# Two projection blocks in one PSUM bank, urgent marks on the delta rule's chain, and tied splits of the last weights

## The chip, the cores and the metric

The kernel runs on one core of a Trainium2 chip. TensorE (PE) does the matrix products, VectorE (DVE) and ScalarE (ACT) the elementwise work, GpSimd (POOL) some fills, and SyncE (SP) issues most DMAs. Every engine takes its instructions in the order of its own queue and waits on semaphores that others raise. The metric is device microseconds of one launch, the median of several runs.

## The reference

One layer of a hybrid network on 256 tokens of 2048 features, all in fp32:

```python
h = rms_norm(x, attn_norm_w)
proj = h @ w_in                       # 3360 columns for the RWKV half, 3088 for the delta rule's half
y_a = rwkv7_mixer(proj[..., :N_RWKV_IN], ...)       # token shift, low-rank gates, recurrence over tokens
y_b = gdn_mixer(proj[..., N_RWKV_IN:], ...)         # causal conv of 4 taps, gated delta rule in chunks of 64
x = x + concat([y_a, y_b]) @ w_out
h = rms_norm(x, ffn_norm_w)
x = x + (silu(h @ ffn_w_gate) * (h @ ffn_w_up)) @ ffn_w_down      # 5632 inner columns
return rms_norm(x, final_norm_w)
```

The delta rule walks four chunks in order. In each it forms the new values from the state `S`, adds to the output, and updates `S`, so that a chunk can't begin before the one ahead has left its state. At its end stand a norm of each head, a transpose and a product with `silu(z)`.

## The kernel before, in words

**Weights.** All weights come as fp32 tiles of 128x1024 (512 KB). Each is split into a high part `wh`, a rounded copy made by ACT, and a low part `wl`, the rest, made by DVE; three products (high by high, high by low, low by high) stand for one in fp32. `load_split` (L177) issues the DMA on SP's queue and the split. There are three buffers `raw` and two each of `wh` and `wl`. `split` (L244, lines L246 and L247) takes a whole tile at once; `halves_of` (L194, lines L202 and L203) takes it in two halves, for the FFN.

**First projection.** `proj_in` (L309) makes one column block of 128 output features for 256 tokens: two weight tiles, for the two halves of the 2048 inputs, each with 24 matmuls in `products` (L214: 16 that use `wh`, then 8 that use `wl`). The block fills 256 of the 512 fp32 columns of one PSUM bank, tag `pb`, of which there are two. `evac_norm` (L228, line L232) multiplies the block by `rstd` into one of two buffers `pr`, and a token shift (L238, L239) or a conv of four taps (L667, L669) follows. Blocks come in pairs, `m` = 0 and 1, which fill the two halves of one tile `t`, `outt` or `z`: twelve pairs in `rwkv_stream` (L649), eight in `conv_silu` (L660), four in the loop over `z` (L982), the last of which, `last2`, is built in two banks.

**Side work.** The recurrences are generators. `tick` (L165) is called after each step of `products` and carries each generator as far as its condition lets it, so that its instructions stand between the products in program order. `gdn` (L748) holds the delta rule: `tri_inverse` (L336), then four chunks. In a chunk: `psK` = keys and queries by the state (L898), eight corrections of `vn` (L903), `psUg` (L911), scaled copies (L915, L917), `psSg` for the new state (L923, then L928 or L932), `psOg` (L938, L942, L944), and, after every second chunk, squares with sums (L949), an inverse root (L951, L139 to L143) and a scaling (L954). The last steps transpose to `ps_og` (L964) and write `yg` (L967). Then follow the splits of the four `ys` tiles (L1008), the right-hand sides of the next projection.

**Second projection.** `w_out` is gone through twice (L1015): `q` = 0 for all 16 column blocks needs the RWKV outputs `yR` alone, `q` = 1 needs `yg`.

**FFN.** Eleven units of 512 inner columns, each with a gate and an up product (`gate_up`, L1049, 8 weight tiles and 96 matmuls of 128x512 each) and two `down` (L1134, 4 tiles and 48 matmuls each). The last unit's `down` weights are split ahead of time into SBUF places that others have left: within `gate_up` of the unit at column 36 (b = 0 and 2), at every even `kk` a tile is loaded to the one buffer `raw_end` (L1062), and at the next odd `kk` `halves_of(raw, own)` splits it (L1057, rows named `wend`). These are eight tiles, four in the gate and four in the up product.

**What sets the order.** The kernel is written in program order, and the tile framework's scheduler puts each engine's queue together at build time by simulating the machine: of the instructions that are ready in its model, the one with the lowest priority number goes first. The number is the place in program order; within `hi()` (L60) it is lowered by a million, so that `hi` work goes ahead of all other, and among `hi` work the earlier in the program first. Loads and splits of weights and the evacuations of the projections are `hi`; the delta rule's chain is not. `together` (L63) adds edges that keep a list of instructions in order on their engine; an edge without a semaphore only fixes the order.

Of the kernel before, what the change touches and what calls it, by code (L numbers as in the profile page):

```python
# [49 lines left out]
def trunk_kernel(ctx, tc, xT, vecs, fnw, w_up, a_up, g_up, w_in, w_ab, w_out, w_gu, w_dn, out):  # L50
# [9 lines left out]
    def hi():  # L60
        return tc.high_priority(offset=HI)

# [131 lines left out]
    def halves_of(raw, places, by_k=False):  # L194
        parts = []
        r4 = raw.rearrange("p (c k f) -> p k c f", c=4, k=2)
        for h in range(2):
            wh, wl = places()
            src, oh, ol = raw[:, h * 512:h * 512 + 512], wh, wl
            if by_k:  # L200
                src, oh, ol = r4[:, h], wh.rearrange("p (c f) -> p c f", c=4), wl.rearrange("p (c f) -> p c f", c=4)
            S.activation(oh, src, AF.Copy)  # L202
# [23 lines left out]
    prn = [0]  # L226

    def evac_norm(ps):  # L228

        prn[0] += 1  # L230
        pr = prs[prn[0] % 2]
        V.tensor_tensor(pr[:, 4:260], ps[:, 0:T], rstd, ALU.mult)  # L232
        return pr

    def evac_shift(ps, mu, out):
        with hi():
            pr = evac_norm(ps)
            S.activation(out, pr[:, 4:260], AF.Copy, scale=vec[:, mu + OMU:mu + OMU + 1])  # L238
            shifted[0] = V.scalar_tensor_tensor(out, pr[:, 3:259], vec[:, mu:mu + 1], out, ALU.mult, ALU.add)  # L239
        return pr  # L240
# [68 lines left out]
    def proj_in(cb):  # L309
        return proj([(w_in[cb, q], xk[8 * q:8 * q + 8]) for q in range(2)])  # L310

# [6 lines left out]
    for i in range(2):  # L318
        evac_shift(ps_first[i], VEC["mu_l"] + i, pl[:, i, :])
# [329 lines left out]
    def rwkv_stream(hf):  # L649
        for gr in range(2):  # L650
            for i, (d, mu, tag, nb) in enumerate(((kt, "mu_k", "kt", 2), (rt, "mu_r", "rt", 2), (vt, "mu_v", "vt", 4))):
                f = hf * 4 + gr * 2
                t = rp.tile([P, 2, T], F32, tag=tag, name=f"{tag}{hf}{gr}", bufs=nb)
                for m in range(2):
                    evac_shift(proj_in(2 + ((hf * 2 + gr) * 3 + i) * 2 + m), VEC[mu] + f + m, t[:, m, :])
                vready[(hf, gr)] = shifted[0]
                d[(hf, gr)] = t


    def conv_silu(ti, b0, outt):  # L660
        for m in range(2):
            ps = proj_in(2 * ti + m)
            tb = outt[:, m, :]
            with hi():
                pr = evac_norm(ps)
                c0 = (b0 + m) * 4
                S.activation(tb, pr[:, 4:260], AF.Copy, scale=vc("conv", c0 + 3))  # L667
                for i in range(3):
                    V.scalar_tensor_tensor(tb, pr[:, 1 + i:257 + i], vc("conv", c0 + i), tb, ALU.mult, ALU.add)  # L669
# [78 lines left out]
    def gdn():  # L748
# [136 lines left out]
        for ch in range(NCH):  # L885
# [5 lines left out]
            if ch:  # L891
# [10 lines left out]
                for h in range(8):  # L902
                    ready.append(V.scalar_tensor_tensor(vn[rows, cp, h, :],  # L903
# [13 lines left out]
            ready = [S.copy(vn[rows, cp, m::2, :], u3[m * 64:m * 64 + 64]) for m in range(2)]  # L917
            yield None
            mo, news = [], []
            if ch < NCH - 1:  # L920
# [5 lines left out]
                for i in range(2):  # L926
                    if ch == 0:
                        news.append(S.copy(Sg[:, 4 * i:4 * i + 4, :].rearrange("p h f -> p (h f)"), psS[i]))  # L928
                    else:
                        for j in range(4):  # L930
                            h = 4 * i + j
                            news.append(V.scalar_tensor_tensor(Sg[:, h, :], Sg[:, h, :], egc[:, h, ch:ch + 1],  # L932
# [8 lines left out]
            for m in range(2):  # L941
                S.activation(vn[rows, cp, m::2, :], o3[m * 64:m * 64 + 64], AF.Copy, scale=-1.0)  # L942
            for h in range(8 if ch else 0):
                V.scalar_tensor_tensor(vn[rows, cp, h, :], psK[h // 4][rq, h % 4 * P:h % 4 * P + P],  # L944
                                        GTn[rq, cp, h:h + 1], vn[rows, cp, h, :], ALU.mult, ALU.add)
            if x:
                ss, rs, xh = [rsg[:, o + 8 * cp:o + 8 * cp + 8] for o in (0, 16, 32)]
                for h in range(8):
                    S.activation(junk, vn[:, cp, h, :], AF.Square,  # L949
                                 accum_out=ss[:, h:h + 1])  # L950
                V.scalar_tensor_tensor(xh.rearrange("p (h x) -> p h x", x=2), ss.rearrange("p (h x) -> p h x", x=2),  # L951
                                       0.5 / 128, nq[:, cp::2, None].to_broadcast([P, 4, 2]), ALU.mult, ALU.add)
                rsqrt(rs, xh, "g")
                scaled = [S.activation(vn[:, cp, h, :], vn[:, cp, h, :], AF.Copy, scale=rs[:, h:h + 1])  # L954
# [11 lines left out]
        for i, ps in enumerate(pss):  # L966
            V.scalar_tensor_tensor(yg[:, 2 * i:2 * i + 2, :].rearrange("p h t -> p (h t)"), ps, vc("gnw"),  # L967
# [14 lines left out]
    for i in range(4):  # L982
# [66 lines left out]
    def gate_up(c0, m, tag="pb", beside=None):  # L1049
# [243 lines left out]
```

## Time and profile before

| | us |
|---|---|
| median of 3 runs | 1256.54 |
| lowest and highest | 1255.93, 1258.83 |
| the profiled execution, whole | 1255.44 |
| its span in the profile | 1253.7 |
| first matmul of the second projection (`psb` from `ys`) | 397.97 |
| first matmul of the FFN (`psq`) | 510.03 |

The span is counted from the first instruction to the last; 1.7 us lie around it. Up to about 398 us PE works on the first projection with the recurrences between, up to 510 us on the second, and then on the FFN. The profile's page gives busy time by engine; of the trace, the views used below are the busy time in windows, the waits of one engine, the chain of work that ended last, the timeline of one engine, and the groups of instructions by line. In a timeline, the columns are start and duration in us, engine, line, operation, tiles (written, then read), shapes and count, and in brackets the idle time before it and what ended that.

### The profile page before, as it was taken

The numbers are of one execution on the slowest core, as the hardware profiler recorded it, in microseconds if no ns is written. First come the engines' busy times: TensorE is split into PE (matmuls) and PEld (weight loads), VectorE is DVE, ScalarE is ACT, GpSimd is POOL, SyncE is SP. The second block draws the span as 40 slices with busy tenths as digits, with TensorE's granted clock in tenths as the row PEclk, the third lists the DMA queues.
The fourth block names the chain that finished last, engine by engine and source line by source line (L and its number), as shares of the span: only waits on it lengthen the run. The fifth ranks groups of instructions, "written<-read, shape, count | busy, mean of one in ns | idle before, by whom it ended". The sixth has DMA issues, their size and how long they took to land.

```text
span 1253.7 us, 21133 instructions
## 1 busy us (share of the span) xinstructions
PE 1234.8 (98%) x8134; PEld 1087.0 (87%) x8134; DVE 834.3 (67%) x1635; ACT 651.3 (52%) x1199; POOL 17.8 (1%) x63
## 2 busy tenths in 40 slices
PE   8999999999999999999999999999999999999997
PEld 8999999999999989888888888888888888878886
DVE  7987887977966877565555555555656565665554
ACT  7575665667546456554444444444444444454443
POOL 3000000000000000000000000000000000000000
PEclk9999999999999999999999999999999999999999
DMA  7455665575573445676666666666676666676641
GB/s 248 153 169 179 169 170 149 169 186 139 196 213 118 145 159 186 172 205 194 190 190 197 188 193 192 194 190 196 187 198 182 189 190 195 203 236 193 193 151 67
DMA packets 175702, 226.68 MB, mean 181 GB/s; under 512 B 52273, under 2 KB 144561, under 8 KB 175345
## 3 DMA queue, kind: packets, MB, share of 16 engines
q1 hardware_dynamic: 170896, 221.54, 60.4%
q10 hardware_dynamic: 4560, 2.74, 0.8%
q8 instruction: 64, 1.05, 0.4%
q0 software_dynamic: 144, 1.05, 0.2%
q14 instruction: 38, 0.30, 0.1%
HBM read 218.75 MB, written 4.46 MB: 178 GB/s over the span
## 4 chain that ended last, share of the span: by engine, by line
PE 88%; DVE 5%; DMA 3%; issue 1%; ACT 1%; SPq 0%; ACTq 0%; DVEq 0%
PE psq L1070 37%; PE psd L1147 17%; PE psb L220 16%; PE psb L223 8%; DVE wl L247 2%; PE psT L1102 1%; DMA sX_r<-X_r 1%; DMA raw_end<-in_w_dn 1%; DMA st_r<-sX_r 1%; PE ps_A L485 1%; PE psd L1198 1%; PE psd L1196 1%; PE psd L1197 1%; DMA A_g<-sG 0%; PE psSg L923 0%
## 5 line engine op out<-in xcount | busy, mean ns | idle before, releaser
L203 DVE TENSOR_TENSOR wl<-raw,wh 128x512 fp32r<-128x512 f32 x524 | 340.7, 692 | 273.5 <-ACT wh L202 271.8
L202 ACT ACTIVATE wh<-raw 128x512 fp32r<-128x512 f32 x524 | 302.5, 626 | 363.9 <-PE psq L1070 192.4
L1070 PE MATMUL psq<-wh,x2s 128*128 128x512 f32 x1408 | 377.4, 390 | 0.8 <-ACT wh L202 0.8
L1070 PEld LDWEIGHTS psq<-wh,x2s 128*128 128x128 f32 x1408 | 263.7, 188 | 56.2 <-ACT wh L202 1.7
L1070 PE MATMUL psq<-wl,x2s 128*128 128x512 f32 x704 | 217.2, 389 | 0.0
L220 PE MATMUL psb<-xs,wh 128*128 128x256 f32 x816 | 206.4, 287 | 2.4 <-ACT wh L202 1.7
L223 PE MATMUL psb<-xs,wh 128*128 128x256 f32 x816 | 206.0, 286 | 0.0
L1147 PE MATMUL psd<-wh,h 128*128 128x512 f32 x640 | 203.2, 391 | 1.0 <-ACT wh L202 1.0
L246 ACT ACTIVATE wh<-raw 128x1024 fp32r<-128x1024 f32 x128 | 135.4, 1058 | 87.4 <-PE psb L223 67.8
L247 DVE TENSOR_TENSOR wl<-raw,wh 128x1024 fp32r<-128x1024 f32 x128 | 156.1, 1220 | 11.1 <-ACT wh L246 10.9
L220 PEld LDWEIGHTS psb<-xs,wh 128*128 128x128 f32 x816 | 156.8, 192 | 4.4 <-ACT wh L202 2.4
L223 PEld LDWEIGHTS psb<-xs,wh 128*128 128x128 f32 x816 | 156.8, 192 | 1.2 <-issue 0.7
L1070 PEld LDWEIGHTS psq<-wl,x2s 128*128 128x128 f32 x704 | 132.0, 188 | 27.6
L1147 PEld LDWEIGHTS psd<-wh,h 128*128 128x128 f32 x640 | 119.2, 188 | 25.8 <-ACT wh L202 1.7
L220 PE MATMUL psb<-xs,wl 128*128 128x256 f32 x816 | 127.1, 287 | 0.9 <-DVE wl L247 0.7
L1147 PE MATMUL psd<-wl,h 128*128 128x512 f32 x320 | 124.6, 389 | 0.0
L220 PEld LDWEIGHTS psb<-xs,wl 128*128 128x128 f32 x816 | 109.8, 192 | 2.8 <-DVE wl L247 1.1
L1147 PEld LDWEIGHTS psd<-wl,h 128*128 128x128 f32 x320 | 60.1, 188 | 12.7
L223 PE MATMUL psb<-ys,wh 128*128 128x256 f32 x256 | 64.6, 288 | 2.5 <-DVE ys L247 2.5
L220 PE MATMUL psb<-ys,wh 128*128 128x256 f32 x256 | 64.8, 289 | 0.2 <-ACT ys L246 0.2
L223 PEld LDWEIGHTS psb<-ys,wh 128*128 128x128 f32 x256 | 50.1, 196 | 2.8 <-DVE ys L247 2.7
L1155 DVE TENSOR_TENSOR acc<-acc,psd 128x512 f32<-128x512 f32 x80 | 49.5, 682 | 1.8 <-PE psd L1147 1.8
(315 smaller groups left out, 1026.8 us busy)
## 6 DMA issues: line engine op xcount, KB each, us to landing
raw<-in_w_gu SPq DMA_DIRECT2D x176, 512.0 KB, 4.9
raw<-in_w_in SPq DMA_DIRECT2D x99, 512.0 KB, 3.5
raw<-in_w_dn SPq DMA_DIRECT2D x80, 512.0 KB, 4.3
raw<-in_w_out SPq DMA_DIRECT2D x32, 512.0 KB, 3.5
raw_end<-in_w_dn SPq DMA_DIRECT2D x8, 512.0 KB, 4.2
xraw<-in_xT SPq DMA_DIRECT2D x8, 256.0 KB, 5.8
x<-in_xT SPq DMA_DIRECT2D x1, 2048.0 KB, 9.7
raw<-in_w_ab SPq DMA_DIRECT2D x2, 512.0 KB, 4.9
```

The costliest lines, as they stand in the source:

```text
L202: S.activation(oh, src, AF.Copy)
L203: V.tensor_tensor(ol, src, oh, ALU.subtract)
L220: PE.matmul(ps[:, 0:T], w, rt[:, ri, 0:T], start=(first and k == 0 and not low), stop=(last and k == 7 and low == 1))
L223: PE.matmul(ps[:, 0:T], w, rt[:, ri, T:], start=False, stop=False)
L246: S.activation(hi_ap, src, AF.Copy)
L247: V.tensor_tensor(lo_ap, src, hi_ap, ALU.subtract)
L485: PE.matmul(psA[h][:, ch, :], bk[hr, ch].rearrange("p a t -> p (a t)"), ar[hr, p, ch].rearrange("p a t -> p (a t)"), start=True, stop=True)
L1070: last = PE.matmul(banks[tb], t[:, ri, o + tb * P:o + tb * P + P], w, start=(k == 0 and o == 0 and w is wh), stop=(k == KB - 1 and w is wl))
L1102: ms.append(PE.transpose(ps[b][:, o:o + P], sg[tb][:, (2 * b + i) * P:(2 * b + i) * P + P], ident))
L1147: m = PE.matmul(banks[tb * 2 + cg], st, parts[cg][w], start=(i == 0 and w == 0 and st is hh), stop=(i == n - 1 and st is hl))
L1155: V.tensor_tensor(acc[:, tb, cs], acc[:, tb, cs], banks[tb * 2 + cg], ALU.add)
L1196: PE.matmul(ps, hh, wh, start=(i == 0), stop=False)
```

## The change

Three things are changed.

1. `proj_in2` builds the two blocks of a pair in the two halves of one bank, the first block whole and then the second. One `evac_norm` of 128x512 takes both to one buffer `prs` of two halves. The shifts and convs, and the `z` product, then follow for both. `last2` stays as it was. The buffers `pr0` and `pr1` become the halves of `prs`.
2. DVE and ACT instructions of the delta rule's chain and of its end get `hi` priority, by the wrappers `HV` and `HS`; `rsqrt` in it is put under `hi()` too. PE's instructions, `tri_inverse` and the recurrences of the RWKV half are left as they were.
3. `halves_of` keeps a list of ACT's split instructions. With `behind=True`, which the splits of `raw_end` alone pass, each is put after the latest split on ACT's queue.

```diff
+    class Urgent:
+        def __init__(self, engine):
+            self.engine = engine
+        def __getattr__(self, name):
+            op = getattr(self.engine, name)
+            def call(*args, **kw):
+                with hi():
+                    return op(*args, **kw)
+            return call
+
+    HV, HS = Urgent(V), Urgent(S)
...
-    prs = [cp_.tile([P, 260], F32, name=f"pr{i}") for i in range(2)]
-    for pr in prs:
-        G.memset(pr[:, 0:4], 0.0)
+    prs = cp_.tile([P, 2, 260], F32, name="prs")
+    G.memset(prs[:, :, 0:4], 0.0)
...
+    acts = []
+
-    def halves_of(raw, places, by_k=False):
+    def halves_of(raw, places, by_k=False, behind=False):
...
-            S.activation(oh, src, AF.Copy)
+            o = S.activation(oh, src, AF.Copy)
+            if behind:
+                together([acts[-1], o])
+            acts.append(o)
             V.tensor_tensor(ol, src, oh, ALU.subtract)
...
+    def proj_in2(cb):
+        ps = pm.tile([P, 512], F32, tag="pb", name="psb")
+        for m in range(2):
+            for q in range(2):
+                products(ps[:, m * T:m * T + T], load_split(w_in[cb + m, q], whole=True), xk[8 * q:8 * q + 8],
+                         q == 0, q == 1)
+        return ps
...
     def evac_norm(ps):
-        prn[0] += 1
-        pr = prs[prn[0] % 2]
-        V.tensor_tensor(pr[:, 4:260], ps[:, 0:T], rstd, ALU.mult)
-        return pr
+        V.tensor_tensor(prs[:, :, 4:260], ps.rearrange("p (m t) -> p m t", m=2), rstd[:, None, :].to_broadcast([P, 2, T]),
+                        ALU.mult)
+
+    def shift(pr, mu, out):
+        S.activation(out, pr[:, 4:260], AF.Copy, scale=vec[:, mu + OMU:mu + OMU + 1])
+        shifted[0] = V.scalar_tensor_tensor(out, pr[:, 3:259], vec[:, mu:mu + 1], out, ALU.mult, ALU.add)
...
-                for m in range(2):
-                    evac_shift(proj_in(2 + ((hf * 2 + gr) * 3 + i) * 2 + m), VEC[mu] + f + m, t[:, m, :])
+                ps = proj_in2(2 + ((hf * 2 + gr) * 3 + i) * 2)
+                with hi():
+                    evac_norm(ps)
+                    for m in range(2):
+                        shift(prs[:, m], VEC[mu] + f + m, t[:, m, :])
...
-        for m in range(2):
-            ps = proj_in(2 * ti + m)
-            tb = outt[:, m, :]
-            with hi():
-                pr = evac_norm(ps)
+        ps = proj_in2(2 * ti)
+        with hi():
+            evac_norm(ps)
+            for m in range(2):
+                tb, pr = outt[:, m, :], prs[:, m]
...
-                    ready.append(V.scalar_tensor_tensor(vn[rows, cp, h, :],
+                    ready.append(HV.scalar_tensor_tensor(vn[rows, cp, h, :],
...
-                    V.tensor_tensor(vs[rows, m::2, :], u3[m * 64:m * 64 + 64],
+                    HV.tensor_tensor(vs[rows, m::2, :], u3[m * 64:m * 64 + 64],
...
-                    S.activation(junk, vn[:, cp, h, :], AF.Square,
+                    HS.activation(junk, vn[:, cp, h, :], AF.Square,
...
-                rsqrt(rs, xh, "g")
-                scaled = [S.activation(vn[:, cp, h, :], vn[:, cp, h, :], AF.Copy, scale=rs[:, h:h + 1])
+                with hi():
+                    rsqrt(rs, xh, "g")
+                scaled = [HS.activation(vn[:, cp, h, :], vn[:, cp, h, :], AF.Copy, scale=rs[:, h:h + 1])
...
-            V.scalar_tensor_tensor(yg[:, 2 * i:2 * i + 2, :].rearrange("p h t -> p (h t)"), ps, vc("gnw"),
+            HV.scalar_tensor_tensor(yg[:, 2 * i:2 * i + 2, :].rearrange("p h t -> p (h t)"), ps, vc("gnw"),
...
-        for m in range(2):
-            ps = last2[m] if i == 3 else proj_in(42 + 2 * i + m)
+        if i < 3:
+            ps = proj_in2(42 + 2 * i)
             with hi():
-                V.tensor_tensor(z[:, m, :], ps[:, 0:T], rstd, ALU.mult)
-                if m:
-                    S.activation(z, z, AF.Silu)
+                V.tensor_tensor(z, ps.rearrange("p (m t) -> p m t", m=2), rstd[:, None, :].to_broadcast([P, 2, T]),
+                                ALU.mult)
...
-                    wend[ends[2 * q + kk // 2]] = halves_of(raw, own)
+                    wend[ends[2 * q + kk // 2]] = halves_of(raw, own, behind=True)
```

L917, L928, L932, L942, L944 and L951 change in the same way from `V` to `HV` and from `S` to `HS`.

More of the change, by code (lines that the diff above doesn't have):

```diff
@@ L224, in products, with evac_shift @@
             tick()
-    prn = [0]
     def evac_norm(ps):
-        prn[0] += 1
-        pr = prs[prn[0] % 2]
-        V.tensor_tensor(pr[:, 4:260], ps[:, 0:T], rstd, ALU.mult)
-        return pr
-    def evac_shift(ps, mu, out):
+        V.tensor_tensor(prs[:, :, 4:260], ps.rearrange("p (m t) -> p m t", m=2), rstd[:, None, :].to_broadcast([P, 2, T]),
[3 more added lines that the diff above has]
+        shifted[0] = V.scalar_tensor_tensor(out, pr[:, 3:259], vec[:, mu:mu + 1], out, ALU.mult, ALU.add)
+    def evac_shift(ps, mu, out, m=0):
         with hi():
-            pr = evac_norm(ps)
-            S.activation(out, pr[:, 4:260], AF.Copy, scale=vec[:, mu + OMU:mu + OMU + 1])
-            shifted[0] = V.scalar_tensor_tensor(out, pr[:, 3:259], vec[:, mu:mu + 1], out, ALU.mult, ALU.add)
+            pr = prs[:, m]
+            V.tensor_tensor(pr[:, 4:260], ps[:, 0:T], rstd, ALU.mult)
+            shift(pr, mu, out)
         return pr
@@ L307, in trunk_kernel @@
     xk = [(xs[k // 4], k % 4) for k in range(KB)]
-    def proj_in(cb):
-        return proj([(w_in[cb, q], xk[8 * q:8 * q + 8]) for q in range(2)])
     def sigmoid(o, x):
@@ L318, in trunk_kernel @@
     for i in range(2):
-        evac_shift(ps_first[i], VEC["mu_l"] + i, pl[:, i, :])
+        evac_shift(ps_first[i], VEC["mu_l"] + i, pl[:, i, :], i)
     S.activation(twa[0:64, :], pl[0:64, 0, :], AF.Tanh)
@@ L914, in gdn @@
                 for m in range(2):
-                    V.tensor_tensor(vs[rows, m::2, :], u3[m * 64:m * 64 + 64],
+                    HV.tensor_tensor(vs[rows, m::2, :], u3[m * 64:m * 64 + 64],
                                      GT[rows, cp, m:8:2][:, :, None].to_broadcast([64, 4, P]), ALU.mult)
-            ready = [S.copy(vn[rows, cp, m::2, :], u3[m * 64:m * 64 + 64]) for m in range(2)]
+            ready = [HS.copy(vn[rows, cp, m::2, :], u3[m * 64:m * 64 + 64]) for m in range(2)]
             yield None
@@ L941, in gdn @@
             for m in range(2):
-                S.activation(vn[rows, cp, m::2, :], o3[m * 64:m * 64 + 64], AF.Copy, scale=-1.0)
+                HS.activation(vn[rows, cp, m::2, :], o3[m * 64:m * 64 + 64], AF.Copy, scale=-1.0)
             for h in range(8 if ch else 0):
-                V.scalar_tensor_tensor(vn[rows, cp, h, :], psK[h // 4][rq, h % 4 * P:h % 4 * P + P],
+                HV.scalar_tensor_tensor(vn[rows, cp, h, :], psK[h // 4][rq, h % 4 * P:h % 4 * P + P],
                                         GTn[rq, cp, h:h + 1], vn[rows, cp, h, :], ALU.mult, ALU.add)
@@ L989, in trunk_kernel @@
                     products(last2[m], load_split(w_in[48 + m, q], whole=True), xk[8 * q:8 * q + 8], q == 0, q == 1)
-        for m in range(2):
-            ps = last2[m] if i == 3 else proj_in(42 + 2 * i + m)
+        if i < 3:
+            ps = proj_in2(42 + 2 * i)
             with hi():
-                V.tensor_tensor(z[:, m, :], ps[:, 0:T], rstd, ALU.mult)
-                if m:
-                    S.activation(z, z, AF.Silu)
+                V.tensor_tensor(z, ps.rearrange("p (m t) -> p m t", m=2), rstd[:, None, :].to_broadcast([P, 2, T]),
+                                ALU.mult)
+        else:
+            for m in range(2):
+                with hi():
+                    V.tensor_tensor(z[:, m, :], last2[m][:, 0:T], rstd, ALU.mult)
+        with hi():
+            S.activation(z, z, AF.Silu)
         zs[i] = z
```

7 lines of the change are left out of this document (3 added, 4 removed).

## The prediction

> **What bounds the kernel now.** I read the page first, then the busy time in windows, whose columns are the stretch and its length, the busy time (and instructions) of PE, PE's weight loads, DVE, ACT and POOL, the granted clock of TensorE, DMA's share and GB/s.
>
> ```profile
> span 1253.7 us, 21133 instructions
> PE 1234.8 (98%) x8134; PEld 1087.0 (87%) x8134; DVE 834.3 (67%) x1635; ACT 651.3 (52%) x1199; POOL 17.8 (1%) x63
> ```
>
> ```profile
> 20.00:372.00 352.00, 348.70 (x3624) 333.81 (x3622) 291.81 (x722) 211.93 (x421) 12.54 (x27) 1.00 0.59 173
> 372.00:455.00 83.00, 83.00 (x695) 78.41 (x696) 61.54 (x139) 46.38 (x91) 0.00 (x0) 1.00 0.43 136
> ...
> 459.40:462.50 3.10, 0.55 (x3) 0.35 (x3) 3.10 (x6) 1.90 (x3) 0.00 (x0) 1.00 0.53 172
> ...
> 463.80:467.20 3.40, 3.40 (x19) 3.40 (x19) 0.40 (x1) 0.00 (x0) 0.69 (x1) 0.52 0.29 99
> ...
> 467.20:1088.50 621.30, 621.30 (x2965) 522.97 (x2965) 364.77 (x576) 297.70 (x509) 0.00 (x0) 1.00 0.67 191
> 1088.50:1112.73 24.23, 22.39 (x97) 17.46 (x96) 15.23 (x25) 12.83 (x24) 0.00 (x0) 1.00 0.81 261
> 1112.73:1223.00 110.27, 110.27 (x494) 91.33 (x495) 65.53 (x104) 52.31 (x91) 0.00 (x0) 1.00 0.62 182
> ```
>
> PE is the bound almost everywhere. The change neither adds nor takes away a matmul, so it can win only time in which PE stands still or runs slowly. Between 20 us and 1223 us there are three such places: 352.00 - 348.70 = 3.3 us scattered over the first projection, a hole at 459 us with a slow stretch behind it, and 24.23 - 22.39 = 1.8 us in one gate product at 1088 us. From 372 to 455 us, where the marked chain runs, PE has no idle time at all. What PE waits for in the second and third place:
>
> ```profile
> PE psb L223 <- DVE ys L247: 2.5, 1, 2.5
> ...
> PE psd L1147 <- ACT wh L202: 1.0, 1, 1.0
> PE psq L1070 <- ACT wh L202: 0.8, 2, 0.5
> ```
>
> The hole is a wait for the split of `ys`, the end of the delta rule. The gate's are waits for ordinary weight splits on ACT.
>
> **The urgent chain.** DVE's and then ACT's timeline over the chain's last 18 us:
>
> ```profile
> 450.33 0.16 DVE L951 SCALAR_TENSOR_TENSOR rsg<-rsg,nq 128x8 f32<-128x8 f32 x1
> ...
> 451.14 0.17 DVE L143 SCALAR_TENSOR_TENSOR rsg<-rsqrt,rsg 128x8 f32<-128x8 f32 x1
> ...
> 452.15 1.22 DVE L247 TENSOR_TENSOR wl<-raw,wh 128x1024 fp32r<-128x1024 f32 x1
> ...
> 454.09 0.17 DVE L143 SCALAR_TENSOR_TENSOR rsg<-rsqrt,rsg 128x8 f32<-128x8 f32 x1
> ...
> 458.61 1.22 DVE L247 TENSOR_TENSOR wl<-raw,wh 128x1024 fp32r<-128x1024 f32 x1
> 459.74 2.06 DVE L967 SCALAR_TENSOR_TENSOR vnknSg<-ps_og,vec,zs 128x512 f32<-128x512 f32 x3
> ```
>
> ```profile
> 444.49 0.31 ACT L949 ACTIVATE junk<-vnknSg 128x128 f32<-128x128 f32 x1
> ...
> 445.38 1.04 ACT L246 ACTIVATE wh<-raw 128x1024 fp32r<-128x1024 f32 x1
> ...
> 447.93 1.04 ACT L246 ACTIVATE wh<-raw 128x1024 fp32r<-128x1024 f32 x1
> ...
> 449.52 0.19 ACT L949 ACTIVATION_READ_ACCUMULATOR junk<-vnknSg 128x1 f32 x1
> ...
> 454.63 2.45 ACT L954 ACTIVATE vnknSg<-vnknSg,rsg 128x128 f32<-128x128 f32 x8
> ```
>
> Weight splits stand inside the chain. Eleven small DVE instructions of the root go from 450.33 to 454.26 us; the first five of them take 451.31 - 450.33 = 0.98 us, so eleven need 2.2 us, and 3.93 - 2.2 = 1.7 us go to a split and an addition between. The eight squares take 449.71 - 444.49 = 5.2 us with two splits of 1.04 us inside: 2.1 us. The split at 458.61 us stands between `yg`'s first quarter and the other three: 459.74 - 458.61 = 1.1 us. Marked urgent, these dependent instructions are ready as soon as the one before is, and go ahead of any later split: 1.7 + 2.1 + 1.1 = 4.9 us earlier. The hole needs 2.5 us, and 0.2 us more for the high part just before (3.10 - 0.55 = 2.55 us in the window). So it closes with some 2 us to spare, without counting the earlier chunks. Next on PE's path is then PE itself.
>
> Behind the hole the clock counts. From 463.80 to 467.20 us it is granted at 0.52: 3.40 x 0.48 = 1.6 us. It is 1.00 in each long window around, and I take the drop for a consequence of the hole. This place is worth 2.7 + 1.6 = **4.3 us**; bounds 0 (hole stays) and 4.3.
>
> The Trainium skill, "TensorE: Matmul & The Clock Gate", section "Why this matters for your kernels", says that idle gaps over about 3 us put PE back to half the clock. The gap here is shorter, 2.5 us, and the half clock follows all the same. By the row the place gives 4.3 us; by the rule as stated this gap is not the cause, and it would give 2.7 us.
>
> What urgency costs: the splits wait instead.
>
> ```profile
> 500.43 1.08 PE psb L220 x9
> 503.31 1.08 PE psb L220 x9
> ```
>
> ```profile
> L246 ACT ACTIVATE wh<-raw 128x1024 fp32r<-128x1024 f32 x128 | 135.4, 1058 | 87.4 <-PE psb L223 67.8
> L247 DVE TENSOR_TENSOR wl<-raw,wh 128x1024 fp32r<-128x1024 f32 x128 | 156.1, 1220 | 11.1 <-ACT wh L246 10.9
> L944 DVE SCALAR_TENSOR_TENSOR vnknSg<-psK,GTn,vnknSg 64x128 f32<-64x128 f32 x24 | 8.4, 348 | 1.4 <-ACT vnknSg L942 0.8
> L669 DVE SCALAR_TENSOR_TENSOR csv<-pr,vec,csv 128x256 f32<-128x256 f32 x24 | 11.4, 477 | 0.0
> L232 DVE TENSOR_TENSOR pr<-psb,rstd 128x256 f32<-128x256 f32 x43 | 18.0, 421 | 7.0 <-PE psb L220 6.8
> L1155 DVE TENSOR_TENSOR acc<-acc,psd 128x512 f32<-128x512 f32 x80 | 49.5, 682 | 1.8 <-PE psd L1147 1.8
> ```
>
> PE uses a weight tile for 503.31 - 500.43 = 2.88 us. With two `wh`, the next split can begin when PE turns to the tile before it, so ACT has 2.88 - 1.06 = 1.8 us of slack. The low part is needed two thirds into its tile, 1.92 us later: DVE has 2.88 + 1.92 - 1.06 - 1.22 = 2.5 us. The squares in one piece hold ACT for 5.2 - 2.1 = 3.1 us, 1.3 us over its slack, twice; eight corrections hold DVE for 8 x 0.348 = 2.8 us, 0.3 us over. Both bite only if the piece begins just as a split falls due; `L954` holds ACT for 2.45 us now, and PE does not wait. I take 0.3 us; the bounds are 0 and the price of the slower rival below.
>
> **The pairs.** 43 - 3 = 40 evacuations of 421 ns and 6 alike for `z` go: 46 x 421 ns = 19.4 us of DVE. 23 of 128x512 come. No row shows just that; the nearest by size and source is the addition at L1155, 682 ns: 15.7 us, and DVE saves 3.7 us. The bounds are one small evacuation (421 ns, saving 9.7 us) and two (842 ns, saving nothing). PE's matmuls, SP's DMAs and their order stay; that writing a bank's upper half costs PE the same I take for granted at the same shape. The bank must be free a pair later, 4 x 2.88 = 11.5 us, against 0.7 us of evacuation.
>
> But both blocks' results come after the second block. For a shift pair that is 682 - 421 ns and one more 0.48 us, 0.7 us later; for a conv 0.26 + 3 x 0.477 = 1.7 us. Does the delta rule begin later for it?
>
> ```profile
> 348.97 0.82 ACT L744 ACTIVATE vnknSg<-ps_vn,nk 128x256 f32<-128x256 f32 x2
> ...
> 375.57 0.26 ACT L385 COPY TTg<-psO_g 32x128 f32<-32x128 f32 x1 [1.48 <-DVE TTg L385]
> ```
>
> No: its first product needs the last values (L744, done at 349.8 us) and the inverse (L385, done at 375.8 us), so values that are 1.7 us late stay hidden behind 26 us. And a conv leaves DVE a burst of 0.68 + 6 x 0.477 = 3.5 us instead of two of 1.9 us, 1.0 us over DVE's slack if a split stands behind all of it: at worst 8 conv pairs x 1.0 = 8 us. A split is usually ready while the burst still waits for ACT, so I count on none of this, and of the 3.3 us idle in this stage I take **0.5 us** back for the freed DVE time. Bounds: 3.3 us won, 8 us lost.
>
> **The tie.** The chain of waits over the gate, then ACT's timeline:
>
> ```profile
> 1022.32 21.76 PE psq L1070 x96
> ...
> 1088.50 10.89 PE psq L1070 x48
> ...
> 1100.13 4.07 DMA raw_end<-in_w_dn
> ...
> 1106.21 4.77 DMA raw_end<-in_w_dn
> ...
> 1157.54 2.49 PE psq L1070 x11
> ```
>
> ```profile
> 1098.14 1.16 ACT L202 ACTIVATE wend<-raw_end 128x512 fp32r<-128x512 f32 x2 [3.30 <-DMA raw_end<-in_w_dn]
> 1099.20 1.14 ACT L202 ACTIVATE wh<-raw 128x512 fp32r<-128x512 f32 x2
> ```
>
> One unit takes 1088.50 - 1022.32 = 66.18 us, this one 1157.54 - 1088.50 = 69.04 us: 2.86 us lost. ACT's queue has a `wend` split that waits 3.30 us for its DMA, and behind it stands the `wh` that PE needs next. A tile goes round from issue to issue in 1106.21 - 1100.13 = 6.1 us, while PE needs only 2 weight tiles x 12 matmuls x 21.76/96 = 5.44 us. With the tie each `wend` comes after the `wh` of the even step. ACT and DVE finish that pair some 3.2 us after that `wh` begins, `raw_end` is issued, and 4.1 to 4.8 us later it has landed, at about 7.4 us; the next `wend` may go at 5.44 + 1.16 = 6.6 us. So ACT still waits, about 0.8 us, but the split behind it is due only at 8.16 us (3 x 2.72), and PE needs it another 2.72 us later. The slip grows by about 1 us from tile to tile, three times, so the last may just be late. SP issues the load of the next `raw` behind `raw_end`; it has over 1 us to spare. Two of the eight tiles that are now split before the gate join the others, four in the gate and four in the up product, where DMA has 0.62 of its time used. I keep 0.5 us of the loss: **2.4 us** won; bounds 0 and 2.86, and below it PE's three waits for `wh`, 1.8 us, in eight places, 4.8 us, so 3 us lost.
>
> **Sum.** 4.3 - 0.3 + 0.5 + 2.4 = 6.9 us less. The profiled execution took 1255.44 us, 1.7 us around its span, which gives 1248.5 us. It was 1.1 us below the median of the runs shown, 1256.54 us; against that I predict **1249.6 us**, with 2 us either way for this case alone. A difference of 0.2%, 2.5 us, is about what a measurement of this kernel tells from none.
>
> **The rivals.**
> *The hole stays.* PE's queue is laid out by a model, and if that puts `ps_og` no earlier, the chain's gain is idle time on DVE. For it: from 372 us on PE's products, not DVE's, could be what the chain waits for; against it: the three splits above stand in the last 18 us, where little PE work is left in the chain. Only the tie and the pairs count: -2.4 - 0.5 + 0.3, 1253.9 us, at the border of measurable. 0.14.
> *The tie moves the wait.* ACT still waits for `raw_end`, now in eight places: -4.3 + 0.3 - 0.5, 1252.0 us. 0.13.
> *The slow clock stays.* If something other than the hole halves it, 1.6 us of the gain fail to come: 1251.2 us. This is what the skill's rule for a gap this short would allow. 0.04.
> *Splits starve.* Slower: the corrections of one chunk and those of the next follow each other on DVE with only `psK` between, 2 x 8 x 0.35 = 5.6 us, and a `wl` behind both is 5.6 - 2.5 = 3.1 us late. This is a hole like the one at 459 us, with its 1.6 us of slow clock: 4.7 us each. The state's update and the corrections meet likewise, so there are four such places. From two on, 9.4 us, it outweighs the 6.9 us: 1259.1 us with two, 1263.8 us with three. For it: no wait is left to absorb it, since PE has no idle time there; against it: DVE is busy 61.54 of 83 us in that window, and a split can slip in wherever the chain waits for PE or ACT. 0.15.
> *Nothing to see.* The edits don't order the queues as they say, or conv bursts eat the gain: within 2 us of 1256.5. 0.06.
>
> **Chances and range.** The forecast has 0.48. Faster by over 0.2%: 0.48 + 0.13 + 0.04 and half of the first rival, 0.72. The same: the other half and the last, 0.13. Slower: 0.15. For the low end, all waits go: 4.3 + 2.86 + 3.3 = 10.5 us, 1246.0 us. The high end takes in the last rival: 1257.5 us. The starved splits and a little below the low end are left out.
>
> **What would show it.** Right: no wait of PE for `ys` L247, clock 1.00 from 455 to 480 us, the root's instructions in one piece on DVE, the unit of the tied splits near 66.2 us, the evacuation at x23 near 0.68 us. Wrong: new waits of PE for `wl` L247 or `wh` L246 between 372 and 455 us, a DVE-released hole after a conv, waits of ACT for `raw_end` that PE shares, or `ps_og` no earlier than now.

## The result and the profile after

The changed kernel took 1265.81 us in the median of 5 runs (1263.05 to 1267.9), the kernel before beside it 1258.49 us (1255.93 to 1259.82): a ratio of 1.0058 with a 95% interval of 1.0039 to 1.0077. It is slower, and the prediction of 1249.6 us was wrong in size and in sign. The profiled execution of after took 1263.05 us against 1255.44 us, 7.6 us more.

The page's first lines after, then PE's longest wait (engine, line, what it waited for, us in total, times, longest):

```profile
span 1261.3 us, 21106 instructions
...
PE 1235.9 (98%) x8134; PEld 1086.4 (86%) x8134; DVE 834.4 (66%) x1612; ACT 650.8 (52%) x1201; POOL 17.7 (1%) x62
```

```profile
PE ps_og L993 <- ACT vnknSg L73: 7.5, 1, 7.5
```

The hole at 459 us, which was to close, has grown: PE waits 7.5 us for the scaled outputs of the delta rule, where it waited 2.5 us for the split behind them. The busy time in windows, first the stretch around the hole before, then three stretches after:

```profile
455.00:480.00 25.00, 22.26 (x173) 21.82 (x172) 17.80 (x28) 14.36 (x25) 0.69 (x1) 0.93 0.54 184
```

```profile
20.00:372.00 352.00, 347.05 (x3500) 332.31 (x3499) 287.75 (x693) 211.35 (x420) 12.51 (x27) 1.00 0.59 171
372.00:455.00 83.00, 83.00 (x797) 77.72 (x797) 60.29 (x125) 41.55 (x73) 0.00 (x0) 1.00 0.46 140
455.00:480.00 25.00, 17.37 (x137) 16.50 (x134) 17.13 (x38) 15.57 (x38) 0.69 (x1) 0.86 0.35 126
```

From 455 to 480 us PE is busy 22.26 - 17.37 = 4.9 us less, and at a mean clock of 0.86 instead of 0.93 it loses another 0.07 x 25 = 1.8 us. The first projection has 352 - 347.05 = 4.95 us of idle time instead of 3.3, and the tied unit (below) 0.5 us more. That is 8.8 us, some 1 us more than the 7.6 us between the two executions; where that 1 us comes back stays open. The large term is the hole.

Why the hole grew stands on SP's queue and in the groups of instructions by tile (duration in ns, least, median, most, then first and last start). SP's DMA issues before, then after:

```profile
301.15 0.33 SPq L848 DMA_DIRECT2D sG<-gates  x1
302.75 0.33 SPq L184 DMA_DIRECT2D raw<-in_w_in  x1
303.77 2.99 SPq L862 DMA_DIRECT2D A_g<-sG  x6
306.81 0.49 SPq L184 DMA_DIRECT2D raw<-in_w_in  x1
307.34 0.96 SPq L862 DMA_DIRECT2D A_g<-sG  x2
```

```profile
301.52 5.34 SPq L198 DMA_DIRECT2D raw<-in_w_in  x2
307.26 0.33 SPq L876 DMA_DIRECT2D sG<-gates  x1
312.03 0.33 SPq L890 DMA_DIRECT2D A_g<-sG  x1
312.44 0.44 SPq L198 DMA_DIRECT2D raw<-in_w_in  x1
312.93 5.62 SPq L890 DMA_DIRECT2D A_g<-sG  x6
318.65 0.44 SPq L198 DMA_DIRECT2D raw<-in_w_in  x1
319.13 0.43 SPq L890 DMA_DIRECT2D A_g<-sG  x1
```

The last input of the inverse, `A_g`, is issued at 319.6 us instead of 308.3. Before, its way there is: keys' conv (`kT`), transposes (`ps_kn`), gates (`ps_gb`), products of keys (`ps_kq`), the store `sG`, the loads `A_g`. The steps of that way in both kernels, starts in us:

| | before | after | later by |
|---|---|---|---|
| last `kT` of the keys' conv | 266.2 | 269.6 | 3.4 |
| first `ps_gb` | 275.5 | 280.6 | 5.1 |
| `sG` stored | 301.2 | 307.3 | 6.1 |
| `tmp_g`, first step of the inverse | 313.7 | 323.6 | 9.9 |
| `psF_g`, behind the inverse | 364.3 | 379.7 | 15.4 |
| first `psUg`, the delta rule's chain | 371.6 | 387.0 | 15.4 |

In RWKV's half the first `psF_r` comes at 195.5 instead of 186.3 us, so the lateness is there from the first recurrence on; the last `psF_r`, of its second inverse, comes at 292.3 instead of 275.3 us, and the work behind it stands on the same queues as the delta rule's. The inverse's 31 steps on DVE take some 41 us before and 42 us after. From the last step to `psF_g` it is 9.6 us before and 14.3 us after; on that way the result goes to DRAM and back by SP's queue. So a delay of 3.4 us at the keys has become 15.4 us at `psUg`, and these traces do not tell how much of it each queue adds.

### The profile page after: what moved, and what is told of

Read it like the earlier page. It is cut to its first block, busy times and chain, and to the rows that moved or that the text cites. A ratio compares the mean times of both kernels' runs of the same rounds, so it can differ in the third digit from the quotient of the medians.

```text
span 1261.3 us, 21106 instructions
## 1 busy us (share of the span) xinstructions
PE 1235.9 (98%) x8134; PEld 1086.4 (86%) x8134; DVE 834.4 (66%) x1612; ACT 650.8 (52%) x1201; POOL 17.7 (1%) x62
## 4 chain that ended last, share of the span: by engine, by line
PE 84%; DVE 8%; DMA 3%; ACT 2%; issue 2%; SPq 1%; DVEq 0%; ACTq 0%
PE psq L1104 36%; PE psd L1181 17%; PE psb L248 15%; PE psb L251 7%; DVE wl L275 2%; DMA raw_end<-in_w_dn 1%; PE psT L1136 1%; DMA A_r<-sA 1%; PE psd L1232 1%; PE psd L1231 1%; PE psd L1230 1%; DVE X_r L379 1%; DVE tmp_r L377 0%; PE psSg L951 0%; DMA sX_r<-X_r 0%
## 5 line engine op out<-in xcount | busy, mean ns | idle before, releaser
L275 DVE TENSOR_TENSOR wl<-raw,wh 128x1024 fp32r<-128x1024 f32 x128 | 155.9, 1218 | 19.4 <-ACT wh L274 17.9
L1181 PEld LDWEIGHTS psd<-wl,h 128*128 128x128 f32 x320 | 60.1, 188 | 12.6
L248 PE MATMUL psb<-ys,wh 128*128 128x256 f32 x256 | 63.3, 285 | 0.0
L251 PE MATMUL psb<-ys,wh 128*128 128x256 f32 x256 | 63.1, 285 | 0.1
```

The lines of the kernel that those rows point to most:

```text
L248: PE.matmul(ps[:, 0:T], w, rt[:, ri, 0:T], start=(first and k == 0 and not low), stop=(last and k == 7 and low == 1))
L251: PE.matmul(ps[:, 0:T], w, rt[:, ri, T:], start=False, stop=False)
L275: V.tensor_tensor(lo_ap, src, hi_ap, ALU.subtract)
L1181: m = PE.matmul(banks[tb * 2 + cg], st, parts[cg][w], start=(i == 0 and w == 0 and st is hh), stop=(i == n - 1 and st is hl))
```

## The experiments

Each ratio is to runs of the kernel before on the same chip, with its 95% interval; it goes by all runs and is not the quotient of two medians. Lines differ between kernels by some tens.

**The three parts alone.** Each was put into the kernel before by itself, and the last two together:

```diff
 e1_pairs:      + proj_in2, evac_norm, prs; V and S in the chain, no tie
 e2_urgent:     + HV, HS and hi() around rsqrt in the chain
 e3_tie:        + halves_of(raw, own, behind=True)
 e4_urgent_tie: + both of these
```

> Only part 1 of the change: pairs in one bank, no urgent marks, no tie. Theory A (the pairs make the delta rule's inverse late): psUg begins near 387 us as in the changed kernel, the chain from there keeps its old 86 us, so ps_og comes near 473 us and PE's hole at the end of the first pass of w_out grows to 12 to 14 us; the kernel is slower than before by 10 to 16 us, more than the whole change (+7 us). Theory B (the urgent marks or the tie cost the time): psUg begins near 372 us, within 2 us of before.

> Only part 2: urgent marks, blocks in banks of their own, no tie. Theory A: psUg begins at 371 to 372 us as before, the chain from psUg to ps_og shrinks from 85.7 to about 80 us, PE no longer waits for ys and the clock stays at 1.00: 4 us faster than before. Theory B (splits starve behind the urgent work): new waits of PE for wh or wl between 372 and 455 us, no faster than before, or slower.

> Only part 3: the tie. Theory A (the round of one raw_end buffer, 6 us, is too long whatever the order): the unit with the tied splits takes 68.5 to 69.6 us as in the changed kernel (69.0 before), the time is within 1 us of before. Theory B (the tie works, something else of the change spoils it): the unit takes 66.2 to 66.7 us, 2.4 us faster.

> Parts 2 and 3 without the pairs. Theory A: the sum of the two alone, 4 us faster than before, with the unit of the tied splits as in e3. Theory B (the tie is worth 2.4 us): 6 to 7 us faster.

| | median us | ratio |
|---|---|---|
| e1_pairs | 1264.68 | 1.004 (1.0027 to 1.0053) |
| e2_urgent | 1258.7 | 0.9998 (0.9986 to 1.0009) |
| e3_tie | 1259.41 | 1.0001 (0.999 to 1.0013) |
| e4_urgent_tie | 1259.39 | 0.9995 (0.9985 to 1.0005) |

The pairs carry the loss (their 1.004 and the whole change's 1.0058 have intervals that overlap): with them alone `psUg` begins at 389.5 us and PE waits 7.7 us at `ps_og`. The expected hole of 12 to 14 us and loss of 10 to 16 us were too high: they let the chain keep its 86 us, and it takes 469.6 - 389.5 = 80.1 us where PE is through with the products ahead of `ps_og` before the chain is done. The other two parts do nothing that can be measured. That is not because they gain and lose alike: the places at which they were aimed have not moved. First DVE's timeline of e2_urgent through the root and the writing of `yg`, then the two groups of PE before that mark the chain's first product and its end, then the same two of e2_urgent:

```profile
457.49 0.17 DVE L158 SCALAR_TENSOR_TENSOR rsg<-rsqrt,rsg 128x8 f32<-128x8 f32 x1
457.57 0.41 DVE L1035 TENSOR_TENSOR x<-x,psb 128x256 f32<-128x256 f32 x1
457.90 0.16 DVE L156 SCALAR_TENSOR_TENSOR rsqrt<-rsg 128x8 f32<-128x8 f32 x1
457.98 1.22 DVE L262 TENSOR_TENSOR wl<-raw,wh 128x1024 fp32r<-128x1024 f32 x1
459.12 0.16 DVE L157 TENSOR_TENSOR rsqrt<-rsqrt,rsg 128x8 f32<-128x8 f32 x1
...
463.75 1.41 DVE L73 SCALAR_TENSOR_TENSOR vnknSg<-ps_og,vec,zs 128x512 f32<-128x512 f32 x2
465.08 1.22 DVE L262 TENSOR_TENSOR wl<-raw,wh 128x1024 fp32r<-128x1024 f32 x1
```

```profile
L911 PE MATMUL psUg<-vnknSg,TTg x64: 269/269/320, 371.6 to 438.2; 64*64 64x128 f32 x64
...
L964 PE MATMUL ps_og<-ident,vnknSg x16: 271/272/273, 457.3 to 458.9; 128*128 128x128 f32 x16
```

```profile
L926 PE MATMUL psUg<-vnknSg,TTg x64: 269/269/320, 377.4 to 443.1; 64*64 64x128 f32 x64
...
L980 PE MATMUL ps_og<-ident,vnknSg x16: 271/272/273, 463.1 to 464.8; 128*128 128x128 f32 x16
```

The weight split of 1.22 us still stands inside the root, and another between the quarters of `yg`, though the chain is marked. And the chain takes 463.1 - 377.4 = 85.7 us, as before (457.3 - 371.6 = 85.7). (e2_urgent's profiled execution is later by some 6 us throughout that part; up to the chain its instructions stand in the same order as before.) In both kernels `ps_og` stands on PE's queue behind all products of the second projection's first pass, and PE has no idle time in that stretch, so with the queue in this order a faster DVE could not have brought it forward. In e2_urgent it is DVE that waits for PE along the chain, not the other way round:

```profile
DVE vnknSg L73 <- PE psK L913: 5.1, 1, 5.1
```

Nor do the marks gain anything where PE does wait for the chain's end: from `psUg` to `ps_og` it takes 467.1 - 387.0 = 80.1 us in the changed kernel, with them, and the same 80.1 us in e1_pairs, without them. The root's eleven instructions stand in one piece of 2.2 us in both.

**The inverse marked urgent.** If the late start is the cause, bringing the inverse forward should help both kernels. All its instructions and DMAs for the delta rule were marked:

```diff
+        V_, S_, Y_, G_ = [Urgent(e) if nm == "g" else e for e in (V, S, SY, G)]
```

> The kernel before with one edit: the instructions and DMAs of the delta rule's inverse (tri_inverse of g, with its loads and stores) are urgent; no pairs, no urgent chain, no tie. Theory A (the hole at the end of the first pass of w_out is set by when the delta rule begins, that is by the inverse): the inverse's 62 DVE steps take less than the 40 us of before, psUg begins 5 to 20 us earlier than 371.6 us, PE's wait for ys goes, and with it the half clock: 4 us faster than before. Theory B (the chain's place in PE's queue is tied to the products whatever it starts from): ps_og stays behind all 384 products of the first pass and the hole stays 2.5 us: no change.

> The changed kernel, all three parts, with the same edit on the inverse. Theory A (the pairs cost time only by making the inverse late): psUg comes 5 to 20 us earlier than 387 us, the hole of 7.5 us shrinks to 0 to 3 us, and the kernel is within 0.2% of before or faster, instead of 0.6% slower. Theory C (the pairs cost time elsewhere too, in the first projection): the hole shrinks but the kernel stays 3 us or more slower than before.

f1_inv (on before): 1262.1 us, 1.0038 (1.0025 to 1.0052). f2_after_inv (on after): 1266.43 us, 1.0076 (1.0058 to 1.0093). Both were no help, and f1_inv is slower than before. The marks brought the loads of `Bd_g`, which are wanted only after the inverse, to the same rank as `A_g`: SP issued three `A_g`, three `Bd_g`, one `A_g`, five `Bd_g` and only then the last four `A_g`, at 314.3 us instead of 308.3. The inverse's first step came 3.6 us late, at 317.3 us, and `psUg` 7.1 us late, at 378.7 us; PE waited 5.1 us at `ps_og`, and the time rose by 5.0 us. In f2_after_inv `psUg` stayed at 387.1 us and the hole at 7.5 us. So the experiment failed at its aim, but f1_inv shows the same link without any pair: some loads 6 us later in a queue, the chain's start later, the hole longer, the kernel slower.

**Only some of the pairs.** f3_conv_pairs has them for the eight conv pairs alone, f4_shift_z_pairs for the twelve shift pairs and the first three of `z`.

```diff
 f3:  shifts and z as before:  + for m in range(2): evac_shift(proj_in(...), ...)
 f4:  convs as before:         + for m in range(2): ps = proj_in(2 * ti + m) ...
```

> Part 1 for the eight conv pairs alone; the shift blocks and z blocks go to banks of their own as before; no urgent marks, no tie. Theory A1 (the bursts of six conv steps on DVE, beside the preparation of the inverse, make it late): sG is written 4 to 8 us later than at 301 us and psUg begins 8 to 15 us later than 371.6; slower by 0.3 to 0.5%. Theory A2 (any pair does it, through the order of the queues): psUg within 3 us of before here.

> Part 1 for the twelve shift pairs and three z pairs alone; conv blocks as before; no urgent marks, no tie. Theory A1: psUg within 3 us of 371.6 us and no change in time. Theory A2: psUg 8 to 15 us late, slower by 0.3 to 0.5%.

f3_conv_pairs: 1269.21 us, 1.0095 (1.0078 to 1.0112), `psUg` at 391.8 us, PE's wait 7.9 us. f4_shift_z_pairs: 1265.59 us, 1.007 (1.0052 to 1.0087), 383.9 us, 5.1 us. Either half is as dear as the whole or dearer, so the loss is no sum over the pairs. In f3 the first `psF_r` is at 187.6 us, nearly as before, and only the way from the keys on is late; in f4 `psF_r` is already at 196.0 us. The last step of the keys' conv is 10.0 us late in f3 (276.2 us) and `psUg` 20.2 us; in f4, where the convs are as before, `psUg` is 12.3 us late all the same. So neither expectation holds, which gave the lateness to one kind of pair: two different starts of it end in the same hole. In f3 PE also waits 2.2 us for an evacuation to `prs`; why it is slower than all pairs together I can't say in full.

**Only the lateness.** g1_late has the old banks and the old evacuations of 128x256. Only the shift or conv of a pair's first block waits for the second block's evacuation:

```diff
+    both.append(evac_norm(ps, done))        # each block, as before
...
+    a = S.activation(out, pr[:, 4:260], AF.Copy, scale=vec[:, mu + OMU:mu + OMU + 1])
+    together([a], after)                    # after = the second block's evacuation, for m = 0
```

> The kernel before, with the old banks and the old evacuations, but the shift or conv of a pair's first block held back until the second block's evacuation is done (twelve shift pairs, eight conv pairs). Nothing is computed otherwise. Theory 'late results' (the pairs are slow because the recurrences, the gates and with them the delta rule's inverse get their first block's results a block later): the first psUg after 383 us instead of 371.6, a hole of PE of 5 to 8 us ahead of or at ps_og, 1262 to 1267 us, ratio 1.003 to 1.008. Rival 'bank and width' (the sharing of one bank, or the evacuation of 128x512 that goes with it, is what costs): start and time as before, psUg 371 to 374, ratio within 0.002 of 1.

1264.55 us, 1.0036 (1.0021 to 1.0051). The waits and the group of `psUg`:

```profile
PE ps_og L981 <- ACT vnknSg L971: 7.7, 1, 7.7
```

```profile
L928 PE MATMUL psUg<-vnknSg,TTg x64: 269/269/320, 385.3 to 451.9; 64*64 64x128 f32 x64
```

Without a shared bank or a wide evacuation the start is 13.7 us late, the hole as long and the ratio as high as with the pairs. The order on PE's queue moves alike, too: counted in products of the projections that stand ahead of it, the first `ps_gb` is at 1730 before and at 1789 both after and in g1_late, and `psUg` at 2292, 2404 and 2388. The lateness of the first block's results is enough without bank and width. One other thing came along in g1_late, the six conv steps in a row on DVE; but f4 has no such row and is late as well.

The way of the delay is not that of the table alone. In g1_late the last step of the keys' conv is only 1.0 us late (267.2 us), `sG` 6.0 us and `psUg` 13.7 us, while the last `psF_r` of RWKV's half comes at 290.8 us, 15.5 us late. In f3 it is the keys that are late and RWKV's half is not. So the delay reaches the inverse by its own inputs and by work of the other half on the same queues; the share of each is not settled.

**The loads in one piece.** The store `sG`, the loads `A_g`, the store `sX_g` and the loads `st_g` were marked urgent, `Bd_g` not: g2_pairs_loads on the pairs alone, g3_before_loads on the kernel before.

```diff
-        SY.dma_start(out=sG, in_=bgm.rearrange("p h c t -> p (h c) t"))
+        Urgent(SY).dma_start(out=sG, in_=bgm.rearrange("p h c t -> p (h c) t"))
...
-                        SY.dma_start(out=A[p0:p0 + 16],
+                        Urgent(SY).dma_start(out=A[p0:p0 + 16],
```

> The pairs alone, with the delta rule's store sG, its loads A_g, the store sX_g and the loads st_g marked urgent on SP's queue, so that no weight load stands between the A_g (in the pairs alone they go from 312.3 to 319.7 us, with two weight loads between). Theory 'the queue of SP carries part of the delay': the last A_g some 2 to 3 us earlier, the inverse and psUg 3 to 5 us earlier (384.5 to 387 instead of 389.5), hole 5 to 6 instead of 7.7, ratio to before 1.001 to 1.003 instead of 1.004. Rival 'all of it is the late keys': start within 1 us of 389.5 and ratio 1.004.

> The kernel before with the same four marks and nothing else: its eight A_g go in one piece instead of six and two. Theory 'the start of the delta rule sets the hole': psUg 1 to 2 us earlier than 371.6, the hole of 2.5 us shrinks to 1 or less and with it, perhaps, the half clock behind it, 1253.5 to 1256 us, ratio 0.997 to 0.999. Rival 'the chain stretches to the products that stand between': psUg earlier, but ps_og still behind all 384 products of the first pass, the 2.5 us wait for ys unchanged, ratio within 0.001 of 1.

g2_pairs_loads: 1262.69 us, 1.003 (1.0017 to 1.0043). The inverse begins at 321.2 instead of 324.9 us, but `psUg` only 1.5 us earlier, at 388.0; PE's wait at `ps_og` is 6.3 us. Against the 1.004 of e1_pairs the intervals overlap: SP's queue carries some of the delay, and how much is not settled.

g3_before_loads: 1257.1 us, 0.9971 (0.9956 to 0.9985), faster. PE's timeline around `ps_og`, and PE's busy time over ten of these microseconds:

```profile
458.82 0.64 PE L233 MATMUL psb<-ys,wl 128*128 128x256 f32 x4
459.30 1.91 PE L978 MATMUL ps_og<-ident,vnknSg 128*128 128x128 f32 x16
460.97 0.72 PE L233 MATMUL psb<-ys,wl 128*128 128x256 f32 x4
```

```profile
455.00:465.00 10.00, 10.00 (x87) 9.95 (x85) 7.49 (x11) 7.29 (x13) 0.00 (x0) 1.00 0.40 134
```

There is no hole. By the count of products in the trace, `psUg` stands 10 products earlier on PE's queue, and `ps_og` has moved ahead of the last 28 products of the first pass. They run while `yg` is scaled and split, which is the 2.5 us for which PE stood still. That `psUg` comes 1 to 2 us earlier can't be read from the times: this execution stores `sG` at 305.3 us, some 4 us after that of before, and starts `psUg` at 375.7 us. Nor is its total shorter (1257.43 us against 1255.44 us), as PE is idle for 7.5 us from 20 to 372 us and not for 3.3 us; with the same marks that idle time is 4.4 us in h1_loads_ends_tie below. The gain rests on the twelve runs, whose median is 2.0 us below that of before beside them.

**A second buffer for the last weights.** g4_two_ends is before with the tie and two `raw_end`:

```diff
-                    raw = rp.tile([P, 1024], F32, tag="i1", name="raw_end")
+                    if kk // 2 % 2:
+                        raw = fp.tile([P, 1024], F32, tag="raw2", name="raw_end")
+                    else:
+                        raw = rp.tile([P, 1024], F32, tag="i1", name="raw_end")
```

> The kernel before with the tie and a second buffer for raw_end, so that a load of the last weights can run while the tile before it waits for its splits. Theory 'one buffer's round trip of 6.1 to 6.9 us sets the unit' (against the 5.44 us in which PE uses two weight tiles): no wait of PE for wh in that unit, its length 66.2 to 66.8 us instead of 69.0 to 71.2, 2 to 3 us less, ratio 0.997 to 0.999. Rival 'ACT's queue or the DMA engines set it': the unit stays at 68.5 us or more and the ratio within 0.001 of 1.

1256.66 us, 0.9974 (0.996 to 0.9989). ACT's timeline in the unit of the tied splits, after, where there is one buffer, then DVE's between the two halves of `wend`, and SP's issue of the next tile:

```profile
1092.93 1.15 ACT L218 ACTIVATE wh<-raw 128x512 fp32r<-128x512 f32 x2 [1.50 <-PE psd L1181]
1093.98 1.14 ACT L218 ACTIVATE wend<-raw_end 128x512 fp32r<-128x512 f32 x2
1095.65 1.15 ACT L218 ACTIVATE wh<-raw 128x512 fp32r<-128x512 f32 x2 [0.53 <-PE psd L1181]
1097.91 1.16 ACT L218 ACTIVATE wh<-raw 128x512 fp32r<-128x512 f32 x2 [1.11 <-DVE wend L222]
1102.09 1.16 ACT L218 ACTIVATE wend<-raw_end 128x512 fp32r<-128x512 f32 x2 [3.02 <-DMA raw_end<-in_w_dn]
1103.15 1.14 ACT L218 ACTIVATE wh<-raw 128x512 fp32r<-128x512 f32 x2
```

```profile
1094.80 0.68 DVE L1189 TENSOR_TENSOR acc<-acc,psd 128x512 f32<-128x512 f32 x1
1095.40 0.69 DVE L222 TENSOR_TENSOR wend<-raw_end,wend 128x512 fp32r<-128x512 f32 x1
1096.00 1.28 DVE L1189 TENSOR_TENSOR acc<-acc,psd 128x512 f32<-128x512 f32 x2
1097.20 0.68 DVE L222 TENSOR_TENSOR wend<-raw_end,wend 128x512 fp32r<-128x512 f32 x1
```

```profile
1097.91 0.34 SPq L1096 DMA_DIRECT2D raw_end<-in_w_dn  x1
```

ACT stands 3.02 us at a `wend` for its DMA, with the next `wh` behind it, though the splits are tied. `raw_end` comes free only when DVE has made the second half, and three additions of `down` products stand ahead of that. The chain of work over that unit shows PE's start in it and in the next, after, then g4_two_ends:

```profile
1095.61 2.28 PE psq L1104 x11
...
1165.17 9.97 PE psq L1104 x44
```

```profile
1091.90 2.28 PE psq L1078 x11
...
1158.96 16.09 PE psq L1078 x71
```

With one buffer and the tie the unit takes 1165.17 - 1095.61 = 69.56 us (70.5 in e3_tie), with two buffers 1158.96 - 1091.90 = 67.06 us, where other units take 66.19 us. No split in it waits for `raw_end` any more.

**What is faster than both.** h1_loads_ends_tie joins g3 and g4; h2_loads_ends is the same without the tie.

> The kernel before with the four marks on the delta rule's store and loads, and with the tie and the second raw_end buffer: no pairs, no marks on the chain. If the two gains lie in different places (the hole at 459 us, the tied unit at 1090 us) they add: 3.7 + 3.3 = 7 us less, ratio 0.9935 to 0.996, no hole at ps_og or ys, tied unit 67 us. If they share a cause or the spread at the start takes them, the ratio is 0.997.

> The same without the tie. Theory 'the buffer alone sets the unit': 67 us or less and the same time as with the tie, within 0.001. Rival 'the tie is needed too' (with two buffers but no tie, the splits of raw_end stand ahead of the weight split that PE needs, and wait for their DMA): the unit near 69 us and 2 us more than with the tie.

h1_loads_ends_tie: 1254.0 us, 0.9955 (0.994 to 0.9971), faster than both kernels of the change; PE has no wait over 0.2 us for `ys`, the unit takes 66.6 us. The ratios of g3 and g4 would give 0.9945 together, within its interval, so the two gains may add in full. h2_loads_ends: 1255.64 us, 0.9974 (0.9959 to 0.9989), the unit 67.7 us, with four waits of ACT for `raw_end`, 9.2 us in total. With the tie there is none. So the tie does its work once there is a second buffer, worth some 1.1 us in the unit; in the whole time the two intervals overlap.

## Why the prediction was wrong

**The pairs (term -0.5 us; measured alone +4.5).** The step that failed is the question "Does the delta rule begin later for it?" and its answer, "No". It named the two inputs of the first product, the values and the inverse, and counted the lateness for the values alone. (Their margin is 22 us, not 26: `psUg` starts at 371.6 us, when the first pieces of the inverse are there and its last, done at 375.8 us, is not. That changes nothing.) The inverse hangs on the keys' conv, by way of the gates and SP's queue, and shares its queues with RWKV's half; the same change makes both late. No such margin lies there: `psUg` comes 15.4 us later after. And the lateness was taken as 1.7 us, that of the second block. The first block's results, ready a whole block sooner before (two weight tiles, 5.8 us), now wait for the second too. g1_late shows that this lateness makes the loss without bank and width. The sizes were right: the evacuation of 128x512 was put at 682 ns and took 685, and no wait of PE for an evacuation to `prs` is among those of after. By their groups the evacuations take 17.9 us instead of 21.5, 3.6 us less, though DVE's busy time on the page is 834.4 after 834.3 us; why the saving does not show there stays open. It would have been of no use, since DVE has a third of its time free. The Trainium skill, "Perfetto Trace Analysis", section "Optimizing Scalar/DVE Operations", says that grouping into larger operations can help if the engine is saturated. DVE's 66% says that the condition does not hold here, and the ratio of 1.004 agrees.

**The urgent chain (term -4.3 us; measured 0).** Two steps failed. First, "these dependent instructions are ready as soon as the one before is, and go ahead of any later split". The timeline of e2_urgent shows splits between them all the same. The queue is fixed beforehand, and rank counts only among instructions that are ready then; that a split which is ready goes into the pause between two dependent steps is my reading, which no run shows by itself. Second, and by itself enough, "So it closes with some 2 us to spare" priced the chain on DVE and ACT without asking where `ps_og` stands on PE's queue. That is the first rival, "the hole stays", with the reason given for it there: PE's products are what the chain waits for. It had 0.14. What g3 shows in its place: the hole closes when `ps_og` moves ahead of products on PE's queue, 28 of them there, with the chain's start 10 products earlier.

**The price of urgency (+0.3 us) and the slower rival.** Splits did not starve: PE is busy 83.00 of 83.00 us from 372 to 455 us after, as before. The slower case came, but by a mechanism that was not among the rivals. (Two sums there are off by little: 1249.6 + 9.4 is 1259.0 and not 1259.1 us, with three places 1263.7, and the last rival reaches to 1258.5 us, beyond the high end of 1257.5.)

**The tie (term -2.4 us; measured 0).** The step that failed is "ACT and DVE finish that pair some 3.2 us after that `wh` begins", and with it "So ACT still waits, about 0.8 us". The three additions on DVE's queue, 1.8 us in all, were left out of it: the next tile is issued at 1097.91, 5.0 us after 1092.93. It lands 4.2 us later, as the prediction had it, but that is at 9.2 us, not at 7.4, and ACT has been free since 1099.07, at 6.1 us. So it stands 3.02 us, in front of the next `wh`. This is near the rival "the tie moves the wait", at 0.13, but the waits were there before: six of the eight tiles make ACT wait, 12.6 us in total before and 14.9 us after, where the prediction's timeline showed one. The bound is the round of one buffer, 5.8 to 6.8 us from issue to issue after, against 5.44 us of use. g4 shows it by taking the bound away. It recovers 2.0 us of the unit's 2.86, near the term, for a cause that the term did not name.

**The clock.** That the half clock follows the hole fits most runs: it is gone in g3, and longer after the longer hole. But e4_urgent_tie has the hole of 2.5 us and no half clock, so the term of 1.6 us was in part a matter of chance, as the last section shows.

## What to carry to other kernels

Before results are gathered into larger operations, follow the earliest of them to everything that hangs on it, through DMA queues and other engines, to the next place where the bounding engine waits; here a saving on an engine with time to spare bought nothing against it. An urgent mark reorders only what is ready when the queue is put together, so look first whether the bounding engine's own queue has the end of the chain behind other work; moving a few loads ahead of others can be worth more than marking the chain. And where a transfer has one buffer, compare its round trip with the time in which it is used before moving the wait about.

## What the runs showed of the hardware that was not expected

The half clock comes in pieces. The window from 455 to 480 us in e4_urgent_tie, then in g4_two_ends, both with the hole of 2.5 us, and in g1_late, with 7.7 us:

```profile
455.00:480.00 25.00, 22.26 (x185) 21.82 (x184) 18.80 (x33) 15.68 (x26) 0.69 (x1) 1.00 0.58 200
```

```profile
455.00:480.00 25.00, 22.25 (x162) 21.82 (x162) 16.40 (x29) 13.68 (x24) 0.69 (x1) 0.86 0.63 192
```

```profile
455.00:480.00 25.00, 17.30 (x130) 16.79 (x129) 16.50 (x37) 14.78 (x38) 0.69 (x1) 0.80 0.34 114
```

The mean clocks of 1.00, 0.93, 0.86 and 0.80 that occur here are no, one, two and three stretches of 3.41 us at half speed: 3.41 x 0.5 / 25 = 0.068 each. The same hole of 2.5 us was followed by none (e4_urgent_tie), one (before) or two (g4_two_ends), holes of 7.5 to 7.9 us by two (after, e1_pairs) or three (f2_after_inv, f3_conv_pairs, g1_late). And a shorter gap can be enough: in h1_loads_ends_tie PE waits 1.02 us at 277.2 us for keys (`ps_gb`), has no other gap over 0.15 us in the ten microseconds before, and runs at half clock soon after:

```profile
279.62:283.03 3.41, 3.41 (x58) 3.19 (x61) 3.28 (x9) 2.48 (x4) 0.00 (x0) 0.50 0.42 141
```

The Trainium skill, "TensorE: Matmul & The Clock Gate", section "HAM oscillation — how this bites in real kernels", names a window of 3.4 us for this. The length of a stretch agrees; its limit for the gap, over some 3.4 us, does not, as 2.5 us was enough in most of these runs and 1.02 us in one place. What decides between none and two for the same hole is open; it is worth up to 3.4 us of a single execution (two stretches of 3.41 us at half speed), as much as the gains that were sought here.
